# Rounding part of the in-projection weights on ScalarE in a Hymba-style hybrid decoder layer

## The chip, the cores and the metric

The kernel runs on one core of a Trainium2 chip. The metric is the device time of one execution in microseconds; three runs of the kernel before gave 2929.60, 2932.82 and 2933.56 us, median 2932.82.

TensorE is called PE below, VectorE DVE, ScalarE ACT, GpSimd POOL, and SyncE, which issues the transfers here, SP.

## The reference

One decoder layer over 2048 tokens of width 1024. A single in-projection feeds two parallel head groups, sparse attention and a Mamba-2 (SSD) mixer; their outputs go together through an out-projection, and an MLP of width 4096 follows.

```python
u = rms_norm(h, norm_pre_mix[i])
proj = u @ w_in[i]                      # 1024 x 2636
q, k, v, qi, ki, wi, z, xbc, dt = jnp.split(proj, offsets, axis=-1)
...
attn = sparse_attention(q, k, v, qi, ki, wi, rel_bias)   # top 256 keys by an indexer
ssd = ssd_mixer(z, xbc, dt, ...)                         # conv, chunked scan, gated norm
mix = jnp.concatenate([attn, ssd], axis=-1) @ w_out[i]
h = h + rms_norm(mix, norm_post_mix[i])
f = rms_norm(h, norm_pre_mlp[i]) @ w_mlp_up[i]
f = jnp.square(jax.nn.relu(f)) @ w_mlp_down[i]
h = h + rms_norm(f, norm_post_mlp[i])
```

## The kernel before

**Products.** Every large product is made of three: each operand is split into a high part, which is the value rounded to the format fp32r, and a low part, which is what the rounding left. PE multiplies high by high, high by low and low by high (`mm3`, lines 257, 260 and 261) and sums in PSUM.

**Weights.** `load_w` brings a weight tile in two parts. For each part SP issues the load of the raw tile `wr` (line 246), then `split` makes the high part `wh` (line 229 on ACT or line 231 on POOL, chosen by a flag) and then, always on POOL, the low part `wl = wr - wh` (line 232). `how` is a pair of characters, one flag for each part of a tile; "1" means ACT. There are two buffers for `wh`, two for `wl` and four for `wr`, so the pair of parts that PE works on fills `wh` and `wl`, and a part of the next tile can be rounded only when PE has done the 12 products of each kind that read the part it replaces. The flags of the four weight matrices stand in line 53 of the code as HI_ (in-projection), HO (out-projection), HU and HW (MLP).

**Stages.** The 2048 tokens are four pieces of 512 (t = 0 to 3). The in-projection takes them in order: for each t one narrow tile of mixed columns (`w_misc`, parts of 128x304) and 20 tiles of `w_in` (parts of 128x512): eight for x, B and C of the mixer, two for the indexer's queries, four for the gate z, one for K, one for V, four for the queries of the attention. Each tile is 24 products of 512 columns on PE. Then follow four windows, each an out-projection and an MLP for one t. `p_mm` is the PSUM tile of in-projection and MLP-up products, `p_acc` that of the out-projection, `p_dn` that of MLP-down.

**Work woven in.** Between the products of the in-projection (0 to 763 us in the trace) stand pieces of three other jobs: the SSD mixer of each t (lines 486 to 543), the search for the top 256 keys of query blocks 2 to 8 (`topk`: ACT counts with a Sign activation and an accumulator, line 611; DVE makes the next threshold from the count, lines 618 and 619; 31 steps in turn), and the attention of blocks 0 to 3 (lines 684 to 754). After the z tiles one activation (line 402) applies SiLU to 128x6144 values on ACT; then come the copies of K (line 414). At the end of each t, `row_scale` squares the next piece on ACT (line 283) and `moving` splits the next activations `u` on ACT, DVE and POOL (lines 305 to 312) from raw tiles `xr`, which share the four `wr` buffers.

**Order.** Each engine runs its own list in order; an instruction that waits holds up all behind it. The lists are laid out when the program is built, by a scheduler that places instructions by priority and by its own estimate of when their inputs are there. A changed engine for one operation therefore shifts other instructions too.

Of the kernel before, what the change touches and what calls it, by code (L numbers as in the profile page):

```python
# [41 lines left out]
def hybrid_layer(ctx, tc, x, x_t, w_cols, n_post_mix, n_post_mlp, w_in, w_misc, dt_bias, a_log, d_skip,  # L42
# [7 lines left out]
    dr = ctx.enter_context(tc.tile_pool(name="dr", bufs=1, space=DRAM))  # L50


    HI_, HO, HU, HW = "00,11,00,00".split(",")
    FC, BC = (2,3)
    TB = "acc"
    WL = 2
# [25 lines left out]
    def tl(tag, shape, dt=F32, name=None):  # L82
        pool, bufs, slot = place(tag)
        return pool.tile(shape, dt, tag=name if tag in ("s", "ks", "ssm") else slot, name=name or tag, bufs=bufs)
# [17 lines left out]
    def pt(tag, name=None):  # L102
        pool, bufs, slot = place(tag)
        return pool.tile([P, 512], F32, tag=slot, name=name or tag, bufs=bufs)
# [460 lines left out]
    def load_stack(r0, i, nh, tag):  # L565

        qs = tl(tag, [P, 2, nh, P], F32R, name=tag)
        for var in range(2):
            for part in range(2):
                SP.dma_start(qs[part * DH:(part + 1) * DH, var].bitcast(F32),  # L570
                                 q_d[part ^ var, r0:r0 + nh * DH, i * P:(i + 1) * P].rearrange("(h d) t -> d h t", d=DH))
        return qs

    def topk(i0, g):

        n = (i0 + g) * P
        per = g if g * n <= L else g // 2
        scs = []
        for i in range(i0, i0 + g):
            ni = (i + 1) * P  # L580
            qs = load_stack(0, i, HI, "qi")
            if len(scs) % per == 0:
                rows = tl("sc", [P, per, n])
            sc = rows[:, len(scs) % per, :]
            scs.append(sc)
            for j0 in range(0, ni, 512):
                w = min(512, ni - j0)
                for h in range(HI):
                    p = pt("tp", "p_ix")
                    for var in range(2):  # L590
                        PE.matmul(p[:, 0:w], qs[:, var, h, :], KI[:, j0:j0 + w], start=var == 0, stop=var == 1)  # L591
                    if h == 0:
                        V.tensor_scalar(sc[:, j0:j0 + w], p[:, 0:w], 0.0, wsc[:, i, 0:1], op0=OP.max, op1=OP.mult)
                    else:
                        S.activation(p[:, 0:w], p[:, 0:w], AF.Relu)
                        V.scalar_tensor_tensor(sc[:, j0:j0 + w], p[:, 0:w], wsc[:, i, h:h + 1], sc[:, j0:j0 + w],
                                               op0=OP.mult, op1=OP.add)
                yield
            V.tensor_tensor(sc[:, i * P:ni], sc[:, i * P:ni], cn["caus"], op=OP.add)
            if ni < n:  # L600
                G.memset(sc[:, ni:n], MASKED)

        cnt = tl("ks", [P, 4], name="cnt")[:, 0:g]

        keep = tl("ks", [P, 4], I32, name="keep")[:, 0:g]
        cnd = tl("ks", [P, 4], I32, name="cnd")[:, 0:g]

        def count(bias):

            for j in range(g):  # L610
                S.activation(junk_k[:, 0:n], scs[j], AF.Sign, bias=bias(j), accum_out=cnt[:, j:j + 1])  # L611

        count(lambda j: tiny)
        V.tensor_scalar(cnd, cnt, float(2 * TOPK - n), -1.0, op0=OP.is_lt, op1=OP.mult)
        V.tensor_scalar(cnd, cnd, -1073741824, None, op0=OP.bitwise_xor)
        for b in range(30, -1, -1):
            count(lambda j: cnd[:, j:j + 1].bitcast(F32))
            V.tensor_scalar(keep, cnt, float(2 * TOPK - n), float(1 << b), op0=OP.is_ge, op1=OP.mult)  # L618
            V.scalar_tensor_tensor(cnd, keep, (1 << b) | ((1 << b) >> 1), cnd, op0=OP.bitwise_xor, op1=OP.bitwise_xor)  # L619
            yield  # L620
        thr = tl("ks", [P, 4], name="thr")[:, 0:g]
        aux = tl("ks", [P, 4], name="aux")[:, 0:g]
        mag = tl("ks", [P, 4], I32, name="mag")[:, 0:g]
        V.tensor_scalar(mag, cnd, 0x7fffffff, None, op0=OP.bitwise_and)
        V.tensor_scalar(aux, mag.bitcast(F32), 1.17549435e-38, None, op0=OP.is_ge)
        V.tensor_tensor(mag.bitcast(F32), mag.bitcast(F32), aux, op=OP.mult)
        V.scalar_tensor_tensor(thr, cnd.bitcast(F32), -1.0, aux, op0=OP.mult, op1=OP.mult)
        V.tensor_scalar(aux, mag.bitcast(F32), float(2.0 ** -24 * (1 + 2.0 ** -10)), None, op0=OP.mult)
        for j in range(g):
            i, sc, t1, c1, a1 = i0 + j, scs[j], thr[:, j:j + 1], cnt[:, j:j + 1], aux[:, j:j + 1]  # L630
            mk = tl("mkk", [P, n], BF16)
            eq = junk_k[:, 0:n]
            V.tensor_scalar(mk, sc, t1, None, op0=OP.is_gt, op1=OP.add, accum_out=c1)
            V.scalar_tensor_tensor(a1, c1, float(TOPK), a1, op0=OP.is_ge, op1=OP.mult)
            V.tensor_tensor(t1, t1, a1, op=OP.add)
            V.tensor_scalar(mk, sc, t1, None, op0=OP.is_gt, op1=OP.add, accum_out=c1)
            V.tensor_scalar(c1, c1, -1.0, float(TOPK), op0=OP.mult, op1=OP.add)
            V.tensor_scalar(eq, sc, t1, -1.0, op0=OP.is_equal, op1=OP.mult)
            V.tensor_scalar(mk, sc, t1, -BIG, op0=OP.is_lt, op1=OP.mult)
            yield  # L640
            V.tensor_tensor_scan(sc, eq, eq, c1, op0=OP.add, op1=OP.bypass)
            V.scalar_tensor_tensor(sc, sc, 0.0, eq, op0=OP.is_lt, op1=OP.mult)
            V.scalar_tensor_tensor(mk, sc, BIG, mk, op0=OP.mult, op1=OP.add)
            SP.dma_start(m_d[i, :, 0:n], mk)
            yield
# [319 lines left out]
    def ktask(groups, a, b):  # L965
        n = sum(31 + sum(2 + -(-(i + 1) // 4) for i in range(i0, i0 + g)) for i0, g in groups)
        return "k", chain(*(topk(*e) for e in groups)), n, a, b
# [121 lines left out]
```

## Time and profile before

| | |
|---|---|
| median of three runs | 2932.82 us |
| the profiled execution | 2928.61 us |
| its span, first to last instruction | 2926.8 us |
| PE busy | 2754.8 us, 94% of the span |
| DVE, ACT, POOL busy | 1668.1, 1483.0, 1775.7 us |
| mean granted clock of PE | 0.977 of full speed |
| in-projection, from 0 to the first out-projection product | 763 us |

A row of the trace gives busy time of an engine, the time it sat idle before an instruction, and which engine's work ended that idle time. Matmuls overlap: in an undisturbed stretch a product of 512 columns is listed with 0.39 us, but one starts every 0.23 us.

### The profile page before, as it was taken

How to read it: one execution, taken by the hardware profiler on the slowest of the kernel's cores; microseconds unless marked ns; L12 is line 12 of the kernel's file. 1: busy time of each engine (PE TensorE's matmuls, PEld its weight loads, DVE VectorE, ACT ScalarE, POOL GpSimd, SP SyncE). 2: the span in 40 equal slices, each digit the busy share in tenths (PEclk: the TensorE clock that was granted, in tenths of full speed). 3: DMA queues.
4: the chain of work that ended last, by engine and by line, in shares of the span. 5: the costliest groups of instructions: out<-in, count | busy, mean ns of one | idle time of the engine just before them, and what ended most of it. 6: DMA issues, size and time to landing. Idle time of an engine off the chain costs nothing.

```text
span 2926.8 us, 41172 instructions
## 1 busy us (share of the span) xinstructions
PE 2754.8 (94%) x13558; PEld 2240.5 (77%) x13558; DVE 1668.1 (57%) x4106; ACT 1483.0 (51%) x2550; POOL 1775.7 (61%) x1721
## 2 busy tenths in 40 slices
PE   7988989888889999999899999999999999999998
PEld 5766767666668887888688878878888888778886
DVE  6579688878575656657765565666444342511113
ACT  2475577665746586767683847644332332311101
POOL 4666556667656656564457575644564656578775
PEclk9999999989989999999999999999999999999999
DMA  4754754634733333355233222553232225522222
GB/s 131 233 181 142 228 158 132 214 107 166 243 120 116 111 110 97 101 163 191 97 98 103 92 94 81 164 185 102 87 96 80 93 78 177 204 94 97 95 94 87
DMA packets 286741, 383.46 MB, mean 131 GB/s; under 512 B 26520, under 2 KB 151360, under 8 KB 286528
## 3 DMA queue, kind: packets, MB, share of 16 engines
q1 hardware_dynamic: 286528, 380.84, 40.1%
q8 instruction: 107, 1.75, 0.2%
q14 instruction: 106, 0.87, 0.1%
HBM read 316.44 MB, written 64.30 MB: 130 GB/s over the span
## 4 chain that ended last, share of the span: by engine, by line
PE 68%; DVE 13%; ACT 5%; DMA 5%; POOL 4%; issue 4%; SPq 1%; POOLq 0%; DVEq 0%; ACTq 0%
PE p_mm L261 9%; PE p_mm L257 9%; PE p_mm L260 9%; PE p_dn L261 7%; PE p_dn L260 7%; PE p_dn L257 7%; PE p_o L726 4%; PE p_s L684 4%; PE p_pt L718 3%; ACT junk_k L611 3%; POOL wl L232 2%; PE p_ix L591 2%; PE p_acc L257 1%; PE p_acc L260 1%; PE p_acc L261 1%
## 5 line engine op out<-in xcount | busy, mean ns | idle before, releaser
L232 POOL TENSOR_TENSOR wl<-wr,wh 128x512 fp32r<-128x512 f32 (+1 forms) x740 | 994.9, 1345 | 177.6 <-ACT wh L229 112.6
L231 POOL TENSOR_SCALAR wh<-wr 128x512 fp32r<-128x512 f32 x674 | 448.7, 666 | 727.6 <-PE p_mm L260 339.2
L257 PE MATMUL p_mm<-u,wh 128*128 128x512 f32 (+1 forms) x1696 | 680.4, 402 | 38.2 <-ACT u L311 15.4
L261 PE MATMUL p_mm<-u,wl 128*128 128x512 f32 (+1 forms) x1696 | 679.8, 402 | 13.6 <-POOL wl L232 13.5
L260 PE MATMUL p_mm<-u,wh 128*128 128x512 f32 (+1 forms) x1696 | 670.1, 396 | 0.5 <-POOL u L309 0.3
L611 ACT ACTIVATE junk_k<-sc,cnd 128x512 int8<-128x512 f32 (+10 forms) x434 | 576.4, 1328 | 161.7 <-DVE cnd L619 131.5
L260 PE MATMUL p_dn<-wl,g 128*128 128x512 f32 x1008 | 401.8, 399 | 3.5 <-POOL wl L232 3.5
L257 PEld LDWEIGHTS p_mm<-u,wh 128*128 128x128 f32 (+1 forms) x1696 | 321.3, 189 | 108.6 <-POOL wh L231 19.6
L261 PE MATMUL p_dn<-wh,g 128*128 128x512 f32 x1008 | 399.1, 396 | 2.7 <-POOL g L837 2.7
L261 PEld LDWEIGHTS p_mm<-u,wl 128*128 128x128 f32 (+1 forms) x1696 | 320.2, 189 | 88.4 <-POOL wl L232 22.0
L260 PEld LDWEIGHTS p_mm<-u,wh 128*128 128x128 f32 (+1 forms) x1696 | 320.6, 189 | 69.5 <-DVE u L312 2.1
L257 PE MATMUL p_dn<-wh,g 128*128 128x512 f32 x1008 | 328.7, 399 | 1.3 <-POOL wh L231 0.6
L835 ACT ACTIVATE r<-r 128x512 f32<-128x512 f32 x128 | 80.4, 629 | 434.6 <-DVE r L834 434.1
L689 DVE CUSTOM_DVE_ANT_0 pp<-p_s,mk 128x512 f32<-128x512 f32 (+3 forms) x320 | 192.7, 606 | 135.5 <-PE p_s L684 132.0
L720 ACT ACTIVATE ppt<-p_pt 128x512 fp32r<-128x512 f32 (+1 forms) x288 | 155.7, 567 | 209.4 <-PE p_pt L718 172.6
L721 DVE TENSOR_TENSOR ppt<-p_pt,ppt 128x512 fp32r<-128x512 f32 (+1 forms) x288 | 183.0, 654 | 120.8 <-ACT ppt L720 117.9
L260 PEld LDWEIGHTS p_dn<-wl,g 128*128 128x128 f32 x1008 | 189.9, 188 | 46.5 <-POOL wl L232 5.8
L261 PEld LDWEIGHTS p_dn<-wh,g 128*128 128x128 f32 x1008 | 190.0, 188 | 43.2 <-POOL g L837 3.1
L257 PEld LDWEIGHTS p_dn<-wh,g 128*128 128x128 f32 x1008 | 185.8, 189 | 41.9 <-POOL wh L231 2.9
L726 PE MATMUL p_o<-ppt,VV 128*128 128x256 f32 x1088 | 211.8, 295 | 1.1 <-ACT ppt L720 0.7
L618 DVE TENSOR_SCALAR keep<-cnt 128x1 int32<-128x1 f32 (+1 forms) x341 | 69.7, 204 | 234.9 <-ACT junk_k L611 233.5
L837 POOL TENSOR_TENSOR g<-r,g 128x512 fp32r<-128x512 f32 x128 | 170.1, 1330 | 54.4 <-ACT g L836 53.2
(252 smaller groups left out, 4209.6 us busy)
## 6 DMA issues: line engine op xcount, KB each, us to landing
wr<-w_up SPq DMA_DIRECT2D x256, 256.0 KB, 2.6
wr<-w_down SPq DMA_DIRECT2D x256, 256.0 KB, 2.6
wr<-w_in SPq DMA_DIRECT2D x160, 256.0 KB, 2.9
tq<-toep_d SPq DMA_DIRECT2D x128, 128.0 KB, 2.5
qs<-q_d SPq DMA_DIRECT2D x256, 64.0 KB, 2.4
wr<-w_out SPq DMA_DIRECT2D x64, 256.0 KB, 4.0
mix<-mix_d SPq DMA_DIRECT2D x32, 512.0 KB, 8.5
q_d<-qp SPq DMA_DIRECT2D x24, 512.0 KB, 3.8
```

Of the source, the lines that this page charges most:

```text
L231: G.tensor_scalar(dst_hi, src_f, 1.0, 0.0, op0=OP.mult, op1=OP.add)
L232: G.tensor_tensor(dst_lo, src_f, dst_hi.bitcast(F32), op=OP.subtract)
L257: m = PE.matmul(o, ah, bh, start=first, stop=False)
L260: PE.matmul(o, ah, bl, start=False, stop=False)
L261: state["mm3"] = PE.matmul(o, al, bh, start=False, stop=last).ins.name
L611: S.activation(junk_k[:, 0:n], scs[j], AF.Sign, bias=bias(j), accum_out=cnt[:, j:j + 1])
L684: PE.matmul(p[:, 0:w], qs[:, var, hh, :], K1[:, g, j0:j0 + w], start=var == 0, stop=var == 1)
L689: V.tensor_tensor_reduce(out=pp[:, j0:j0 + w], in0=p[:, 0:w], in1=mk[:, j0:j0 + w], scale=1.0, scalar=-3e38, op0=OP.add, op1=OP.max, accum ...
L720: S.activation(pg[:, 0, 0:w], p[:, 0:w], AF.Copy)
L721: V.tensor_tensor(pg[:, 1, 0:w], p[:, 0:w], pg[:, 0, 0:w].bitcast(F32), op=OP.subtract)
L726: PE.matmul(po[:, c0:c0 + 256], VV[:, kk, g, :], pg[:, part, j * 256:(j + 1) * 256], start=kk == 0 and part == 0, stop=kk == nb - 1 and pa ...
L837: G.tensor_tensor(gt[:, 1, :], r, gt[:, 0, :].bitcast(F32), op=OP.subtract)
```

## The change

In line 53 the flags of the in-projection go from "00" to "10": the high part of the first part of each in-projection weight tile is rounded by ACT (line 229) and no more by POOL (line 231). The second part stays with POOL, and so do both low parts. The narrow tile of t = 0 has flags of its own ("11") and stays as it was. In the built program 83 of POOL's 674 rounding instructions go to ACT, whose own go from 66 to 149; no other engine gets more or fewer instructions. A blank line is left out as well, so that from line 604 on each line number is one less.

```diff
-    HI_, HO, HU, HW = "00,11,00,00".split(",")
+    HI_, HO, HU, HW = "10,11,00,00".split(",")
...
         cnt = tl("ks", [P, 4], name="cnt")[:, 0:g]
-
         keep = tl("ks", [P, 4], I32, name="keep")[:, 0:g]
```

POOL's list in t = 0, at the first tiles of `w_in`, before (`wr` raw, `wh` high, `wl` low part):

```order
L231 TENSOR_SCALAR wh<-wr 128x512
L232 TENSOR_TENSOR wl<-wr,wh 128x512
L231 TENSOR_SCALAR wh<-wr 128x512
L232 TENSOR_TENSOR wl<-wr,wh 128x512
L231 TENSOR_SCALAR wh<-wr 128x512
L232 TENSOR_TENSOR wl<-wr,wh 128x512
```

And after:

```order
L231 TENSOR_SCALAR wh<-wr 128x512
L232 TENSOR_TENSOR wl<-wr,wh 128x512 x2
L231 TENSOR_SCALAR wh<-wr 128x512
L232 TENSOR_TENSOR wl<-wr,wh 128x512 x2
L231 TENSOR_SCALAR wh<-wr 128x512
L232 TENSOR_TENSOR wl<-wr,wh 128x512 x2
```

Of two high parts one is gone; the low part of a tile's first part now stands right behind the low part of the tile before.

ACT's list in t = 1, among the counts of the key search, after (line 610 is line 611 of before: the count; `pp` and `ppt` belong to the attention, `lm` and `cb` to the mixer):

```order
L610 ACTIVATE junk_k,cnt<-sc,cnd 128x512
L229 ACTIVATE wh<-wr 128x512
L736 ACTIVATE ot<-p_o 128x256
L610 ACTIVATE junk_k,cnt<-sc,cnd 128x512 x2
L698 ACTIVATE pp,den<-pp,nm 128x256
L610 ACTIVATE junk_k,cnt<-sc,cnd 128x512
L489 ACTIVATE lm<-lm,adt 128x128 x4
L490 ACTIVATE cb<-cb 128x512
L530 ACTIVATE si<-si 128x256
L610 ACTIVATE junk_k,cnt<-sc,cnd 128x512
L229 ACTIVATE wh<-wr 128x512
```

Between two rounding instructions there stand some ten others, five of them counts; before, none of the two L229 was there.

ACT's list in t = 2, around the long SiLU activation, before:

```order
L530 ACTIVATE si<-si 128x256
L402 ACT_TABLE_LOAD
L402 ACTIVATE pre<-pre 128x6144
L611 ACTIVATE junk_k,cnt<-sc,tiny 128x1024
L414 ACTIVATE K_84<-kk 64x512 x2
L611 ACTIVATE junk_k,cnt<-sc,tiny 128x1024
```

And after:

```order
L229 ACTIVATE wh<-wr 128x512
L402 ACT_TABLE_LOAD
L402 ACTIVATE pre<-pre 128x6144
L530 ACTIVATE si<-si 128x256
L229 ACTIVATE wh<-wr 128x512
L414 ACTIVATE K_84<-kk 64x512 x2
L229 ACTIVATE wh<-wr 128x512
```

The high part of the K tile now stands ahead of the SiLU, that of the V tile behind it.

## Rows read from the trace of the kernel before

**Rows 1.** The page: busy time, share of the span, instructions of each engine

```profile
PE 2754.8 (94%) x13558; PEld 2240.5 (77%) x13558; DVE 1668.1 (57%) x4106; ACT 1483.0 (51%) x2550; POOL 1775.7 (61%) x1721
```

**Rows 2.** By stage: length, busy time of each engine, PE clock, DMA share, GB/s

```profile
45.00:763.00 718.00, 632.78 (x3152) 494.10 (x3152) 560.36 (x1405) 442.99 (x911) 461.54 (x458) 0.96 0.54 171
...
1200.00:2926.00 1726.00, 1676.74 (x8217) 1386.16 (x8215) 812.65 (x1897) 744.36 (x1128) 1029.17 (x984) 0.99 0.35 115
```

**Rows 3.** PE's waits, 45 to 763 us: for whom, us in total, times, longest

```profile
PE p_mm L257 <- POOL wh L231: 11.0, 9, 6.4
PE p_mm L261 <- POOL wl L232: 6.5, 13, 1.1
PE p_y L514 <- DVE ends L492: 6.2, 2, 3.3
PE p_s L684 <- DVE mx L689: 5.3, 5, 2.2
...
PE p_pt L718 <- ACT pp L699: 4.6, 4, 2.5
```

**Rows 4.** POOL by line, 0 to 763 us: busy, mean ns, idle before and releasers

```profile
L232 POOL TENSOR_TENSOR wl<-wr,wh 128x512 fp32r<-128x512 f32 x162 | 221.6, 1369 | 12.7 <-PE p_mm L261 1.0
L231 POOL TENSOR_SCALAR wh<-wr 128x512 fp32r<-128x512 f32 x160 | 111.1, 695 | 115.0 <-PE p_mm L260 93.4 <-DMA wr<-w_in 13.9 <-issue 7.5
```

**Rows 5.** Timeline of POOL in t = 0: start, us, instruction, idle before it

```profile
66.13 0.63 POOL L231 TENSOR_SCALAR wh<-wr 128x512 fp32r<-128x512 f32 x1 [0.71 <-PE p_mm L260]
66.84 1.60 POOL L232 TENSOR_TENSOR wl<-wr,wh 128x512 fp32r<-128x512 f32 x1
68.85 0.62 POOL L231 TENSOR_SCALAR wh<-wr 128x512 fp32r<-128x512 f32 x1 [0.41 <-PE p_mm L260]
```

**Rows 6.** Timeline of PE: two of its waits for a high part

```profile
464.91 0.50 PE L257 MATMUL p_mm<-u,wh 128*128 128x512 f32 x1 [1.46 <-POOL wh L231]
```

```profile
589.06 0.71 PE L257 MATMUL p_mm<-u,wh 128*76 128x512 f32 x1 [6.40 <-POOL wh L231]
```

**Rows 7.** Timelines of SP's queue and of POOL ahead of the wait at 589 us

```profile
584.94 4.01 SPq L246 DMA_DIRECT2D wr<-w_misc  x2
```

```profile
588.57 0.44 POOL L231 TENSOR_SCALAR wh<-wr 128x304 fp32r<-128x304 f32 x1
```

**Rows 8.** DVE by line, 0 to 763 us

```profile
L374 DVE SCALAR_TENSOR_TENSOR pre<-raw,cols,pre 128x512 f32<-128x512 f32 x96 | 88.6, 924 | 3.0 <-ACT pre L372 2.1
L619 DVE SCALAR_TENSOR_TENSOR cnd<-keep,cnd 128x2 int32<-128x2 int32 x93 | 35.4, 380 | 1.4
L618 DVE TENSOR_SCALAR keep<-cnt 128x2 int32<-128x2 f32 x93 | 32.0, 344 | 43.5 <-ACT junk_k L611 43.2
```

**Rows 9.** Lines 374 and 619, 0 to 763 us: ns least, median, most

```profile
L374 DVE SCALAR_TENSOR_TENSOR pre<-raw,cols,pre x96: 714/749/1787, 41.0 to 672.9; 128x512 f32<-128x512 f32 x96
```

```profile
L619 DVE SCALAR_TENSOR_TENSOR cnd<-keep,cnd x105: 143/160/1256, 133.8 to 761.6; 128x2 int32<-128x2 int32 x93, 128x1 int32<-128x1 int32 x12
```

**Rows 10.** Line 229, and what engines at tile p_acc waited for (us, times)

```profile
L229 ACT ACTIVATE wh<-wr x66: 456/623/635, 4.1 to 2528.8; 128x512 fp32r<-128x512 f32 x64, 128x304 fp32r<-128x304 f32 x2
...
  POOL wl L232: 112.6, 46
```

```profile
  POOL wl L232: 3.0, 7
...
  ACT wh L229: 1.9, 3
```

**Rows 11.** Timelines of ACT and DVE around the SiLU of t = 2

```profile
534.72 5.35 ACT L402 ACTIVATE pre<-pre 128x6144 f32<-128x6144 f32 x1 [3.51 <-DVE pre L329]
```

```profile
541.61 0.68 DVE L329 TENSOR_TENSOR kk<-p_mm,rsb 128x512 f32<-128x512 f32 x1
```

**Rows 12.** ACT by line and DVE's longest wait, 0 to 763 us

```profile
L611 ACT ACTIVATE junk_k<-sc,cnd 128x1024 int8<-128x1024 f32 x62 | 70.9, 1144 | 31.1 <-DVE cnd L619 26.8 <-DVE cnd L615 2.0 <-DVE rs_q L219 0.8
```

```profile
DVE keep L618 <- ACT junk_k L611: 50.4, 44, 2.7
```

## The prediction

> **What bounds the kernel now.** The first view is the page's line of busy times: PE is busy for 94% of the span [rows 1], so its products set the length, and a change that moves no product can only move PE's idle time. The second is the table by stage [rows 2]: from 1200 us on PE is busy 97% of the time, but from 45 to 763 us only 632.8 of 718 us, 85 us idle in the very stage that the change touches, at a granted clock of 0.96. The third is the list of PE's waits there [rows 3]. Its 36 rows sum to 80 us: rows ended by DVE sum to 48, by POOL to 17.5, by DMA to 7, by ACT to 6. The reader is to see two things. The two rows on weights, 11.0 and 6.5 us, are all that POOL's weight work costs PE directly, so they bound the direct gain. And the largest share is DVE's, which runs in turn with ACT: its longest wait is for ACT's counts, 50.4 us [rows 12]. ACT is at 443 of 718 us there, POOL at 462, DVE at 560 [rows 2].
>
> The sum is made against the profiled execution, 2928.6 us with a span of 2926.8. That is 4.2 us under the median of the three runs, so 4.2 is added at the end.
>
> **Where the rounding stands now.** In t = 0, before other work is woven in, POOL makes a high part in 0.62 us and a low part in 1.3 to 1.6, then waits 0.41 or 0.71 us for PE to free the next buffer; a part goes by every 2.72 us [rows 5], and PE waits for none. Later POOL also has the mixer's and the attention's work, and comes late 22 times [rows 3]. Over the stage it still waited 93.4 us for PE to free a buffer [rows 4]: mostly it is early.
>
> **The change, part by part.** 80 parts of 128x512 and three of 128x304 move. *What POOL saves* is 83 x 0.62 = 51 us, some 11% of its 462 us in the stage. What of it PE sees is in the two rows on weights. The 6.4 us at 589 us [rows 6] is no rounding: SP stood for 4.0 us over the two loads of that tile's raw parts [rows 7], and the rounding itself was 0.44 us. That leaves 21 waits of 11.1 us in total, the longest 1.46 [rows 6], most around 0.6 us. A queue that is one high part shorter takes at most 0.62 us off each, which cuts five that are longer to a rest of 2 us together: at most 9 us off. Only one part in two is relieved directly; the other finds a shorter queue ahead. I take -6, between 0 and -9.
>
> *What DVE saves.* Small DVE operations are slow in this stage. Line 619 works on two numbers per partition and takes 143 ns at the least, 160 at the median, 1256 at the most [rows 9], 380 in the mean [rows 8]; in the timelines the long ones are those that begin while POOL is at work, and end when it ends. The excess over the short ones is (380 - 160) x 93 = 20 us there, (344 - 160) x 93 = 17 us for line 618 and (924 - 749) x 96 = 17 us for line 374 [rows 8, 9]: 54 us in three groups, perhaps 90 in all, an estimate by the same reading of the smaller groups of that view. POOL's time falls by 11%, so DVE saves 6 to 10 us. PE sees it only where a DVE result is what it waits for, 48 us of 718: from next to nothing (-0.5) to all of it (-10). I take -2, nearer the low end, since most of DVE's small operations are followed by a count on ACT, not by PE.
>
> *What ACT gets.* The same copy takes ACT 0.62 us [rows 10], so 51 us more on 443, 62% to 69% of the stage. Directly PE waits for ACT 6 us; DVE waits for it some 95 us, of which the counts are half [rows 12]. Lengthened by 51/443 = 12%, that is 0.7 us of PE's and 11 us of DVE's; the second is again passed on only in part. Bounds 0 and +12; I take +2, by the same share as for DVE. The Trainium skill (ScalarE: Activation LUTs, Rules for kernel authors) budgets about 0.3 us plus 0.83 ns per element for one activation, which for 512 elements would be 0.73 us and 60 us in all; the row has 0.62, and with 0.73 this term would grow by a fifth, to +2.4.
>
> *What the handover costs.* The new wait is POOL's low part on ACT's high part; queued behind it on POOL are the second part's rounding, the mixer's products (lines 501 to 523) and `qp`. No row shows it in this stage, but the out-projection does it for all of its 64 parts: there POOL waited 112.6 us in 46 waits for ACT, 1.76 us a part, and yet the engines at `p_acc` waited only 1.9 us for the high and 3.0 us for the low parts [rows 10], 0.08 us a part. For 83 parts that would be +6 with PE's weight loads counted in, +2 or so for PE alone. Apart from that there is one place per t that has no likeness in the out-projection: the SiLU of 5.35 us with its table load, behind which V's high part now stands in t = 0, 2 and 3. In t = 2 it ends at 540.1 us; after the 0.4 us of line 530 and 0.62 us of rounding the high part is there at 541.0, the low part at 542.4. K's products are done by 541.6, when DVE takes their sum [rows 11], and V's low part is wanted two products (0.46 us) later, at 542.1: 0.3 us late. In t = 0 and 3 the same reckoning gives 0.4 and 0. So +1 for the three, +9 if each is 3 us late. Together I take +3, between 0 and +15.
>
> *The order.* All lists shift a little from t = 0 on. It moves no work between stages: the in-projection of t = 2 ends at the same place in PE's list as before (2207 instructions from its start) and that of t = 3 twelve later, with one more mixer step ahead of it. A single stall in the stage is 1 to 6 us [rows 3, 6], and which of them stay is chance: 0, with 5 either way. A wait also costs clock: after the wait of 6.4 us a product is listed with 0.71 us where 0.39 is usual [rows 6]; it goes with the waits and is inside those 5.
>
> The sum: -6 - 2 + 2 + 3 = **-3 us**. 2928.6 - 3 = 2925.6 and, moved to the median, **2930 us**. What measurement can tell from no change is 0.2%, 5.9 us, so this is a forecast of no measurable difference.
>
> **The rivals.** *Slower: ACT's list holds the high part back.* A first part may be rounded when PE has done its predecessor, and its low part is wanted 2.72 + 0.46 us later; less 0.62 and 1.3 us of work, 1.3 us are free. ACT serves its list in order, and in t = 2 and 3 that is full of counts of 1024 columns, 1.14 us each and in pairs [rows 12]. The lateness read off the out-projection is 1.76 - 0.62 = 1.1 us a part, just inside the 1.3; from there every microsecond goes to PE. At 0.4 us beyond it on the 42 parts of t = 2 and 3 it costs 17 us, with 3 us at the SiLUs 20; less the 8 saved, +12: 2945. For it: two engines must now be on time, and ACT is the one that others wait for. Against it: 0.08 us a part in the out-projection [rows 10].
>
> *Faster: DVE's stalls count in full.* If the 10 us that DVE saves all lie ahead of PE's 48 us of waits for DVE, the sum is -6 - 10 + 2 + 3 = -11: 2922; with the handover at 0 and POOL's 9 in full, -17: 2916. For it: DVE is the busiest helper of the stage and ends most of PE's waits. Against it: the low parts stay on POOL, and they are two thirds of its weight work and hit DVE for twice as long each. The Trainium skill (SBUF — State Buffer, Who interferes with whom) says that GpSimd and VectorE share one pair of ports under an exclusive lock, that the later one blocks fully, and that ScalarE never waits on anyone; the spread in rows 9 agrees with that, and by that rule alone the move is a gain of this size.
>
> *The change does nothing to PE:* every wait for POOL becomes one for ACT of the same length, 2933. It falls into the forecast's band.
>
> **How the numbers follow.** Forecast and its like (2927 to 2938): 0.40. Slower rival, 2939 to 2950: 0.27. Faster rival, 2914 to 2927: 0.33. The range leaves out the ends of both: 2917 to 2946. Faster by over 0.2%: 0.33; within: 0.40; slower: 0.27.
>
> **What the profile after would show.** POOL's busy time in the first 763 us down by about 51 us, ACT's up by as much. PE's waits for `wh` on POOL down to the 6 us at 589, with a new row `wh` on ACT; that row under 4 us speaks for the forecast, over 12 for the slower rival. The mean of lines 618 and 619 (617 and 618 after) down by a tenth; by a third, with the DVE rows of PE's waits shorter, for the faster one. The start of the out-projection, at 763 us now, at 755 to 768; the stages behind it of the same length within 3 us. The forecast is wrong if that start moves by more than 6 us, or if the time moves behind it, which no term here holds.

## The result: slower by 0.59%

The changed kernel took 2947.13 us (median of 6 runs, 2945.08 to 2956.44), the kernel before 2931.82 us (6 runs, the three given at the start among them, 2925.67 to 2937.26). The ratio is 1.0059, with a 95% interval of 1.0044 to 1.0073. The forecast was 2930 us and no measurable difference; the time lies 17 us above it and 1 us above the range. The profiled execution after took 2945.26 us, with a span of 2943.5.

The first rows of after answer to [rows 1] and [rows 2]: busy time, share and instructions of each engine over the span, then the two stretches (length, busy time of PE, PEld, DVE, ACT and POOL, clock, DMA share, GB/s).

```profile
PE 2764.2 (94%) x13558; PEld 2245.6 (76%) x13558; DVE 1654.7 (56%) x4106; ACT 1519.0 (52%) x2633; POOL 1723.8 (59%) x1638
...
45.00:763.00 718.00, 637.48 (x3185) 498.78 (x3184) 551.01 (x1395) 470.85 (x977) 413.13 (x380) 0.95 0.54 172
1200.00:2926.00 1726.00, 1677.82 (x8189) 1382.95 (x8188) 794.58 (x1837) 729.41 (x1107) 1032.10 (x986) 0.99 0.34 114
```

The instructions moved as said: 83 fewer on POOL and 52 us less of its time, 83 more on ACT and 36 us more (the 83 roundings sum to some 51 us; on ACT neighbouring rows overlap in part). In the stretch that the change touches PE is even busier than before, 637.5 against 632.8 us.

The list of PE's waits from 45 to 763 us answers to [rows 3] (for whom, us in total, times, longest).

```profile
PE p_mm L261 <- POOL wl L232: 14.4, 21, 2.2
PE p_y L514 <- DVE ends L492: 8.1, 1, 8.1
...
PE p_mm L257 <- ACT wh L229: 4.1, 5, 2.0
```

The waits for high parts fell from 11.0 to 4.1 us and those for low parts rose from 6.5 to 14.4: on weights PE waited 17.5 us before and 18.5 after. And here is why, in POOL's and ACT's groups from 0 to 763 us (busy and mean ns, then the idle time before them and what ended it), to be read against [rows 4]:

```profile
L232 POOL TENSOR_TENSOR wl<-wr,wh 128x512 fp32r<-128x512 f32 x161 | 222.5, 1383 | 157.3 <-ACT wh L229 133.8 <-PE p_mm L261 4.9 <-DMA qi<-q_d 4.8
L231 POOL TENSOR_SCALAR wh<-wr 128x512 fp32r<-128x512 f32 x80 | 57.3, 716 | 56.2 <-issue 35.7 <-POOL wl L232 7.8 <-DMA toep_d<-toep 4.8
...
L229 ACT ACTIVATE wh<-wr 128x512 fp32r<-128x512 f32 x81 | 50.3, 621 | 31.2 <-PE p_mm L260 17.0 <-POOL wl L232 7.6 <-issue 6.2
```

Before, the largest share of POOL's idle time was 93 us of waiting for PE to free a buffer, that is, of being early. Now it waits 134 us for ACT's high parts. PE's 21 waits for a low part can be told apart by what POOL did just ahead of that part. In 11 of them, 5.0 us together, POOL had stood for ACT's high part. In eight others, 8.6 us together, it came without a gap from a product of the mixer (lines 501, 504, 523). One of these, in the timelines of POOL and PE after:

```profile
669.42 1.49 POOL L504 TENSOR_TENSOR cb<-cb,si 128x512 f32<-128x512 f32 x1 [3.49 <-DMA si<-s_d]
670.87 1.26 POOL L232 TENSOR_TENSOR wl<-wr,wh 128x512 fp32r<-128x512 f32 x1
```

```profile
672.19 0.50 PE L261 MATMUL p_mm<-u,wl 128*128 128x512 f32 x1 [0.98 <-POOL wl L232]
```

So PE still waits for POOL's own queue, and waits for ACT's are added to it. That the waits for high parts fell is mostly the wait of 6.4 us for `w_misc` [rows 6], which is gone; but hardly any time was won by that. PE came to this place later, behind a wait of 8.1 us for DVE where it had waited 3.3 before, and the first product of `w_misc` starts at 588.0 us against 589.1. Timeline of PE after:

```profile
580.86 0.66 PE L514 MATMUL p_y<-lm,xd 128*64 128x128 f32 x2 [8.14 <-DVE ends L492]
...
588.01 0.71 PE L257 MATMUL p_mm<-u,wh 128*76 128x512 f32 x1 [0.28 <-ACT wh L229]
```

In the whole list of PE's waits in this stretch, the rows ended by DVE sum to 36 us (48 before), those by ACT to 15 (6), those by POOL to 15 (17.5), and all rows to 79 (80). The waits went from DVE to ACT, and the sum stayed.

**Where the time went.** The two traces can be laid side by side by PE's work: for each moment of before, the moment at which after has done the same amount of products (an estimate worked out from the two timelines of PE, each product with its time in an undisturbed stretch). After against before:

| us of before | 225 | 425 | 676 | 775 | 875 | 1326 | 1575 | 1875 | 1970 | 2875 |
|---|---|---|---|---|---|---|---|---|---|---|
| lag, us | +8.2 | +0.6 | -3.5 | -4.9 | +2.1 | +1.4 | +10.7 | +10.7 | +16.3 | +16.3 |

In this pair the in-projection ends with a gain, 7 us are lost between 775 and 875 us, and the rest in three steps up to 1970 us; from there to the end nothing changes. So the whole loss stands behind the stage that was changed, where no operation went to another engine. One thing is mixed into these numbers: of the 16.7 us between the two spans, 7.3 are idle time of PE and 9.4 are busy time, since the same 13558 products ran at a mean granted clock of 0.973 of full speed against 0.977. In the other executions on record the clock was 0.972 to 0.979 before and 0.971 to 0.977 after, so a part of the lag may belong to these two executions and not to the kernels.

The first step is the handover of window 0: the out-projection is done, and the MLP cannot start until DVE has made the residual `xh` (line 802 before, 801 after) and the MLP's operands `u` (line 810 and 809). Timeline of PE before (start, us, instruction, idle before it): the last out-projection product and the first of MLP-up.

```profile
823.65 0.39 PE L261 MATMUL p_acc<-wh,mix 128*128 128x512 f32 x1
...
851.52 0.50 PE L257 MATMUL p_mm<-u,wh 128*128 128x512 f32 x1 [0.33 <-DVE u L810]
```

After:

```profile
822.86 0.39 PE L261 MATMUL p_acc<-wh,mix 128*128 128x512 f32 x1
...
850.54 3.68 PE L806 MATMUL p_tr<-ident,xh 128*128 128x128 f32 x16 [4.47 <-DVE u L809]
...
854.94 0.61 PE L257 MATMUL p_mm<-u,wh 128*128 128x512 f32 x1
```

27.9 us before, 32.1 after. The same stretch by engine, before and after (length, busy time of PE, PEld, DVE, ACT and POOL, clock, DMA share, GB/s):

```profile
823.90:851.50 27.60, 15.43 (x89) 11.65 (x87) 27.12 (x67) 9.36 (x25) 12.51 (x10) 0.69 0.45 159
```

```profile
823.10:854.90 31.80, 18.13 (x91) 14.07 (x91) 31.28 (x90) 15.19 (x36) 8.43 (x10) 0.58 0.34 121
```

DVE is busy for 27.1 of 27.6 us before and for 31.3 of 31.8 after. It sets the length of this stretch, and it has 4.2 us more to do. PE stands idle for 12.2 us of it before and for 13.7 after; the rest of its 4.2 us is that its products run slower, at a mean granted clock of 0.58 against 0.69 of full speed, a mix of its two levels of 1.2 and 2.4 GHz. What DVE did meanwhile, before (its timeline, the rows over 1152 columns):

```profile
816.56 1.41 DVE L633 TENSOR_SCALAR_CACHE_REDUCE mkk<-sc,thr 128x1152 bf16<-128x1152 f32 x1
...
824.05 2.60 DVE L641 TENSOR_TENSOR_SCAN sc<-junk_k,cnt 128x1152 f32<-128x1152 int8 x1
826.69 1.58 DVE L642 SCALAR_TENSOR_TENSOR sc<-sc,junk_k 128x1152 f32<-128x1152 f32 x1
830.51 1.57 DVE L643 SCALAR_TENSOR_TENSOR mkk<-sc,mkk 128x1152 bf16<-128x1152 f32 x1
```

And after:

```profile
837.65 1.40 DVE L635 TENSOR_SCALAR_CACHE_REDUCE mkk<-sc,thr 128x1152 bf16<-128x1152 f32 x1
...
845.12 2.60 DVE L640 TENSOR_TENSOR_SCAN sc<-junk_k,cnt 128x1152 f32<-128x1152 int8 x1
...
848.48 1.34 DVE L641 SCALAR_TENSOR_TENSOR sc<-sc,junk_k 128x1152 f32<-128x1152 f32 x1
849.75 2.71 DVE L809 SCALAR_TENSOR_TENSOR u<-p_tr,cols,u 128x512 fp32r<-128x512 f32 x4
852.72 1.34 DVE L642 SCALAR_TENSOR_TENSOR mkk<-sc,mkk 128x1152 bf16<-128x1152 f32 x1
```

These are the last seven passes of the key search of query block 8 (`topk`, lines 633 to 643 before): they make its mask, which the attention of that block reads later and the MLP does not. Before, four of the seven are over when the out-projection ends. After, all seven, 9.7 us of DVE, lie between the last out-projection product and the first of MLP-up. The place was to be read in DVE's list, of which the diff shows nothing. Before, all seven stand ahead of the first `xh` (the two ends of the piece; the number in front is the line of the list):

```
1480 L633 TENSOR_SCALAR mkk_7527,cnt_5651<-sc_5516,thr_7519 128x1152
...
1496 L643 SCALAR_TENSOR_TENSOR mkk_7527<-sc_5516,mkk_7527 128x1152
...
1512 L802 SCALAR_TENSOR_TENSOR xh_8076<-o_8072,rs1_8878,xh_8076 128x256 x3
```

After, six of the seven stand among `xh` and `u`:

```
1512 L632 TENSOR_SCALAR mkk_7527,cnt_5651<-sc_5516,thr_7519 128x1152
1522 L801 SCALAR_TENSOR_TENSOR xh_8076<-o_8072,rs1_8878,xh_8076 128x256 x3
...
1544 L641 SCALAR_TENSOR_TENSOR sc_5516<-sc_5516,junk_k_79 128x1152
1545 L809 SCALAR_TENSOR_TENSOR u2_8918<-p_tr_8913,cols_75,u2_8918 128x512
...
1550 L642 SCALAR_TENSOR_TENSOR mkk_7527<-sc_5516,mkk_7527 128x1152
```

The key search runs in turn between DVE's threshold and ACT's count. Its counts stand in the same ACT list as the 83 new roundings. It comes later now: the first pass of block 8 starts 53 us after the first out-projection product before, and 70 us after it now. That this delay is the roundings' own, and not the work of the scheduler that laid out the lists anew, is not shown; with the move in t = 3 alone (e12 below) the pass comes earlier than before, 40 us after that product.

### The profile page after: what moved, and what is told of

Same layout as the page of the kernel before. It is cut to its first block, busy times and chain, and to the rows that moved or that the text cites. A ratio compares the mean times of both kernels' runs of the same rounds, so it can differ in the third digit from the quotient of the medians.

```text
span 2943.5 us, 41198 instructions
## 1 busy us (share of the span) xinstructions
PE 2764.2 (94%) x13558; PEld 2245.6 (76%) x13558; DVE 1654.7 (56%) x4106; ACT 1519.0 (52%) x2633; POOL 1723.8 (59%) x1638
## 4 chain that ended last, share of the span: by engine, by line
PE 69%; DVE 12%; DMA 5%; issue 5%; POOL 4%; ACT 3%; SPq 1%; POOLq 0%; DVEq 0%; ACTq 0%
PE p_mm L261 10%; PE p_mm L257 9%; PE p_mm L260 9%; PE p_dn L260 7%; PE p_dn L261 7%; PE p_dn L257 7%; PE p_o L725 4%; PE p_s L683 4%; PE p_pt L717 4%; POOL wl L232 2%; ACT junk_k L610 2%; PE p_ix L591 1%; DVE pre L374 1%; PE p_acc L257 1%; PE p_acc L260 1%
## 5 line engine op out<-in xcount | busy, mean ns | idle before, releaser
L231 POOL TENSOR_SCALAR wh<-wr 128x512 fp32r<-128x512 f32 (+1 forms) x591 | 396.6, 671 | 679.4 <-PE p_dn L261 331.8
L833 DVE SCALAR_TENSOR_TENSOR r<-p_mm,rsb 128x512 f32<-128x512 f32 x128 | 88.0, 689 | 211.7 <-PE p_mm L261 183.8
```

Source lines behind the costliest of these rows:

```text
L231: G.tensor_scalar(dst_hi, src_f, 1.0, 0.0, op0=OP.mult, op1=OP.add)
```

## The experiments

Times are medians; "to before" is the difference to the kernel before as it ran beside that kernel.

### The stage by itself

Both kernels, cut off after the in-projection; copies of the first 128 rows of the input are written out in place of the rest.

```diff
     front.close()
-    state["win"] = "1"
...
-    weave(window(3), [])
```

> The kernel before cut off behind the in-projection stage with the work woven into it: no window, no MLP; the output is 16 copies of rows of x and stands for nothing. It gives the stage a time of its own, some 840 us by the trace (the mixer's last steps end at about 835 us). To be compared with e6 alone.

> The kernel after the change, cut in the same way; the difference to e5 is what the moved rounding does to the stage itself. Theory A (later lists): between -10 and +3 us, since by equal work on PE the profiled run after is 4 us ahead at 775 us. Theory B (the rounding itself): +10 or more.

Measured: 879.38 us for before (875.78 to 881.62), 867.46 after (865.41 to 869.86): 12 us faster with the move. The longest wait of the cut kernel before, 10.3 us for a high part of `w_misc` at the place where the whole kernel before waits 6.4 us [rows 6], is not in the other one. Timelines of PE and POOL there:

```profile
585.90 0.71 PE L257 MATMUL p_mm<-u,wh 128*76 128x512 f32 x1 [10.29 <-POOL wh L231]
```

```profile
585.40 0.44 POOL L231 TENSOR_SCALAR wh<-wr 128x304 fp32r<-128x304 f32 x1 [4.59 <-DMA wr<-w_misc]
```

POOL itself waited there for the load; the rounding is 0.44 us. But this wait is not what the changed kernel gains. There PE comes to the same product at the same time without it, having waited just before for the mixer (5.1, 1.2 and 1.0 us from 574 us on, where the cut kernel before has no other wait). Timeline of PE in e6:

```profile
586.04 0.77 PE L257 MATMUL p_mm<-u,wh 128*76 128x512 f32 x1
```

By equal work of PE (an estimate as above, from the two timelines) it is 1 to 3 us ahead at 600 us, and it gets a lead of some 17 us between there and 680 us, where the cut kernel before has waits of 4.3 and 3.5 us for DVE's results (lines 329 and 225). What follows is only that the move does not make the stage longer; to what the gain belongs is not shown.

### The same comparison in other orders

If the loss belongs to the move, it must stay when the order of the windows is changed by an edit that has nothing to do with it. Four such edits were made to both kernels. Each changes a place in the program from which a task is woven in, adds no operation, and leaves TensorE's list as it is up to the MLP of window 0 or further.

```diff
-    K3, C1, C2, C3 = (-40,760),(-50,355),(355,740),(10,380)
+    K3, C1, C2, C3 = (-30,760),(-50,355),(355,740),(10,380)
```

That is e1 and e2. In e3 and e4 K3 is (-40,740), in e13 and e14 (-50,760); in e15 and e16 C1 and C2 are (-50,365),(365,740).

> The kernel before, with one number of the later weave changed: the key search of blocks 9 to 15 starts at 30 instead of 40 units ahead of the windows. The lists of the in-projection stay word for word as they are on PE; no instruction is added, taken away or moved to another engine. Theory A (the 15 us come from where the later windows' lists happen to put their pieces, not from the rounding): this harmless edit moves the time too, by up to 15 us either way. Theory B (ACT's extra rounding in the in-projection makes the loss): 2932 within 6 us.

> The same number changed in the kernel after the change. Theory A: the difference to the kernel before is no longer +15; anything from -10 to +25, and the difference to e1 too. Theory B: 2947 within 6 us, 15 above e1.

> The kernel before with the end of the same search at 740 instead of 760 units. Theory A: again a shift of up to 15 us either way, of another size than in e1. Theory B: 2932 within 6 us.

> The same in the kernel after the change. Theory A: the difference to e3 is anything from -10 to +25 and not the same as between e2 and e1. Theory B: 2947 within 6 us, 15 above e3.

> The kernel before with the key search of blocks 9 to 15 started ten units earlier in the program (-50 in place of -40): TensorE's list is the same up to the MLP of window 0, no operation is added. Theory (chance of the order behind 850 us): any edit of the order there costs time, because the order of the kernel before happens to be a good one: 2935 to 2955. Rival (the order is worth little): 2930 to 2936, as the kernel before.

> The changed kernel with the same edit. Theory (the move's own loss is the handover of window 0, 5 us; the rest is chance of the order): 0 to 10 us from the kernel before with this edit, on either side of 5; handover 92 to 94 us here against 88. Rival (the move has a loss of 12 or more behind the in-projection of its own): 12 to 20 us above.

> The kernel before with the attention of blocks 5 to 11 ten units later in the program (365 in place of 355): the list is the same up to about 1000 us. Theory (chance of the order): 2935 to 2955. Rival (the order is worth little): 2930 to 2936.

> The changed kernel with the same edit. Theory (handover of 5 us plus chance): 0 to 10 us from the kernel before with this edit. Rival (a loss of its own of 12 or more): 12 to 20 us above.

Measured, with the order as given first:

| order | before, to before | after, to before | after less before |
|---|---|---|---|
| as given | 0 | +15.3 | +15.3 |
| K3 (-30,760): e1, e2 | +12.7 | +23.0 | +10.3 |
| K3 (-40,740): e3, e4 | +1.6 | +21.4 | +19.8 |
| K3 (-50,760): e13, e14 | +31.4 | +25.7 | -5.7 |
| C1 (-50,365): e15, e16 | +8.6 | +19.3 | +10.7 |

Two things follow. An edit that does no work moves the kernel before by 2 to 31 us, always up (the 1.6 of e3 is within the noise): of the five orders its own is the best. And the move costs 10 us in the mean of the five, with a standard error of 4 (from the five differences, which scatter by 9.6 about their mean); from five differences that gives a 95% interval from about -2 to 22, so a loss in every order is likely but not certain. e13 and e14 went against both theories stated for them, with the changed kernel the faster one, and the difference of e15 and e16 lies between the two theories.

The start of the out-projection does not carry the loss. With the C1 pair, the K3 pairs and e7 and e8 (below), six executions on either side share TensorE's list up to there. The first out-projection product comes at 763.4 to 770.1 us in those of before (mean 766.0) and at 761.5 to 774.0 in those of after (mean 767.6). The gain of 2 us in the profiled pair (763.6 to 761.5) is inside that scatter. Nor did the products end earlier. The last in-projection product comes 5 us later after (761.08 against 756.13); before, PE then stood for a transfer of `mix`, which is not so after. Timeline of PE before:

```profile
756.13 0.39 PE L261 MATMUL p_mm<-u,wl 128*128 128x512 f32 x1
...
763.59 1.62 PE L257 MATMUL p_acc<-wh,mix 128*128 128x512 f32 x3 [5.39 <-DMA mix<-mix_d]
```

After:

```profile
761.08 0.39 PE L261 MATMUL p_mm<-u,wl 128*128 128x512 f32 x1
...
761.55 1.06 PE L257 MATMUL p_acc<-wh,mix 128*128 128x512 f32 x3
```

The handover does carry a loss. From the last out-projection product of window 0 to the first of MLP-up the six executions of before take 27.8, 27.9, 28.0, 28.1, 28.3 and 28.3 us, the six of after 31.9, 31.9, 32.0, 32.0, 32.1 and 32.1. The other end repeats too, at no cost: between the last in-projection product and the first of the out-projection the six of before take 4.9 to 7.5 us and the six of after 0.5 to 0.6, but the last in-projection product comes later in those of after, and the out-projection starts no earlier.

### The passes out of the handover

In e9 and e10 six of the seven passes are left out for block 8 alone, so that its mask isn't exact.

```diff
-            V.tensor_scalar(mk, sc, t1, None, op0=OP.is_gt, op1=OP.add, accum_out=c1)
...
+            if i0 != 8:
+                V.tensor_scalar(mk, sc, t1, None, op0=OP.is_gt, op1=OP.add, accum_out=c1)
...
+            else:
+                V.tensor_scalar(mk, sc, t1, -BIG, op0=OP.is_lt, op1=OP.mult)
+                yield
```

> The kernel before, with the key search's last passes (lines 633 to 643) left out for query block 8 alone, so that this block's mask is not exact and the output means nothing. Theory (handover): between the first out-projection product of window 0 and the first MLP-up product PE lives on what VectorE makes; the seven passes over 1152 columns, some 10 us of VectorE, cost PE about 5 us when they stand in that stretch and nothing when they stand ahead of it, as in the kernel before. So here that stretch stays at 88 to 89 us (before: 87.9) and the time within 0.3% of the kernel before. Rival (chance of the order, everywhere): the stretch may be anything from 88 to 94.

> The changed kernel with the same passes of block 8 left out (output means nothing). In the changed kernel they stand among VectorE's instructions for the handover, and the stretch from the first out-projection product to the first MLP-up product takes 93.4 us. Theory (handover): it falls to 88 to 89 here, and the distance to the kernel before falls from 15 to 10 us. Rival (chance of the order): it stays at 92 to 94, since the passes are not its cause.

Measured: 2952.87 us for before (+15.8), 2946.93 for after (+9.8). Timeline of PE in e10, the two ends of the handover:

```profile
823.00 0.39 PE L261 MATMUL p_acc<-wh,mix 128*128 128x512 f32 x1
...
847.92 0.48 PE L257 MATMUL p_mm<-u,wh 128*128 128x512 f32 x1
```

24.9 us, where the changed kernel takes 32.1; in e9 it is 26.7, where the kernel before takes 27.9. From the first out-projection product it is 84.6 us, less than the 88 to 89 expected, and 87.5 in e9. DVE's busy time in this stretch of e10 is 22.7 us, against 31.3. The passes are the cause of the longer handover: without them that of the changed kernel is no longer than the other's. In the whole time e10 is 6 us below e9, and 10 above the kernel before, as expected of it. That e9 came out 16 us above the kernel before, by leaving work out, is put down here to the chance of the order once more, without a run that shows it; it had been expected within 0.3%.

In e17 and e18 the whole search of block 8 goes to the windows, with all of the computation kept.

```diff
-    K0 = 9
+    K0 = 8
```

> The kernel before with the key search of block 8 taken out of the in-projection and put ahead of that of block 9 in the windows, so that its passes stand behind the first handover. Theory (handover): the stretch from the first out-projection product to the first MLP-up product is 85 to 89 us, as before; the time depends on the order of the windows, 2930 to 2955.

> The changed kernel with the same edit. Theory (handover): the stretch is 85 to 89 us here too, the loss of 5 us is gone, and what is left of the move is the gain of the in-projection: the time is 10 us under to 3 us over that of the kernel before with this edit. Rival (a loss of its own in the windows): 8 to 15 us above.

Measured: 2944.11 us for before (10 runs, 2939.04 to 2950.17) and 2944.33 for after (10 runs, 2939.99 to 2951.61), a difference of 0.2. From the first out-projection product to the first of MLP-up it is 83.6 us in e17 and 79.6 in e18, less than the 85 to 89 expected; between the last out-projection product and that, 23.5 and 25.3. With the handover free of the passes in both, the move costs nothing and gains nothing in this pair; by the scatter of 9.6 us above, one pair does not settle it. Both are slower than the kernel before by 9 us, so this is no version to keep.

### Parts of the move

```diff
     def in_proj(t):
         t0 = t * T
+        HI_ = HIS if t in (1, 2,) else "00"
```

with `HIS` the flags "10", and in e12 `t in (3,)`.

> The move for t = 1 and 2 alone; in t = 0 and 3 GpSimd rounds as before. In VectorE's list the passes of block 8 stand ahead of the handover again. Theory (handover, with a real gain inside the in-projection): the stretch from the first out-projection product to the first MLP-up product takes 88 to 89 us; the loss of about 9 us in t = 0 is not made and the gain of t = 1 and 2 stays, so the out-projection begins at 754 to 760 us; the time is 2922 to 2935. Rival (the move costs time wherever it is made, by the longer ScalarE list): the out-projection begins at 762 or later and the time is 2938 to 2948.

> The move for t = 3 alone; the passes of block 8 stand ahead of the handover in VectorE's list. Theory (handover): the stretch from the first out-projection product to the first MLP-up product takes 88 to 89 us, the out-projection begins at 758 to 764, the time is 2924 to 2936. Rival (the move costs time wherever it is made): a quarter of the whole loss, 2936 to 2940, with a stretch of 89 to 91.

Measured: 2961.09 us for t = 1 and 2 (+24.0), 2951.41 for t = 3 (+14.3): neither theory's time. A part of the move costs as much as the whole or more, which no account by tiles allows. On the handover the two fall out as the place of the passes says. In e11 they run from 824 to 842 us, all behind the last out-projection product (824.0), and PE takes 34.6 us from there; so the expectation of a free handover was wrong, because it was read from DVE's list, where they stand ahead of the first `xh`, and not from when they run. In e12 they run from 811 to 825 us, ahead of that product (830.6), and PE takes 22.1, the shortest of all. So the move alone does not put the passes into the handover; the order that comes with it does.

### The passes of blocks 9 to 15 out

In e7 and e8 the passes are left out for the blocks whose search runs in the windows (their masks aren't exact).

```diff
-            V.tensor_scalar(mk, sc, t1, None, op0=OP.is_gt, op1=OP.add, accum_out=c1)
...
+            if i0 < 9:
+                V.tensor_scalar(mk, sc, t1, None, op0=OP.is_gt, op1=OP.add, accum_out=c1)
...
+            else:
+                V.tensor_scalar(mk, sc, t1, -BIG, op0=OP.is_lt, op1=OP.mult)
+                yield
```

> The kernel before without the passes that settle ties in the key search of blocks 9 to 15 (lines 632 to 643 but for one comparison), which leaves out part of the computation. These passes read two SBUF operands on DVE over up to 2048 columns, and POOL's rounding of the MLP weights is up to three times as long beside them. Both theories: faster than before by 10 to 25 us.

> The same passes left out of the kernel after the change. Theory A1 (the later loss is made by these passes meeting POOL's MLP weights at other places): the difference to e7 shrinks to between -6 and +5 us. Theory A2 (the later loss has other causes in the later lists): it stays anywhere, +15 among them. Theory B: +15 as before.

Measured: 2918.16 us for before (-15.8), 2921.60 for after (-12.3), a difference of 3.4 where the kernels as given have 15.3. So leaving out passes that no product of the MLP reads gained 16 us, in spite of a changed order. The 3.4 us are about the handover's 4.1, which is left in this pair. The pair was made to see whether the passes collide with the weights of the MLP on POOL. Timeline of POOL in the changed kernel, in the MLP of window 1, beside the passes of block 13 (which run from 1530 to 1551 us):

```profile
1539.66 7.02 POOL L232 TENSOR_TENSOR wl<-wr,wh 128x512 fp32r<-128x512 f32 x2
...
1549.12 2.91 POOL L232 TENSOR_TENSOR wl<-wr,wh 128x512 fp32r<-128x512 f32 x1
1552.00 0.62 POOL L231 TENSOR_SCALAR wh<-wr 128x512 fp32r<-128x512 f32 x1
1552.70 1.30 POOL L232 TENSOR_TENSOR wl<-wr,wh 128x512 fp32r<-128x512 f32 x1
```

A low part takes 3.5 us beside the passes and 1.3 us behind them, and PE has two waits for one there, 2.4 and 1.8 us. It is one of the steps of the lag (5.7 us between 1525 and 1575). But in the kernel before the same blocks meet too, with a low part of 4.74 us at 1540, and PE was not waiting just then. Whether the fall from 15.3 to 3.4 us is due to these meetings or to chance, one pair cannot tell, since pairs scatter by 9.6.

## Why the prediction was wrong

The step that failed is the order's, "It moves no work between stages": the whole loss came up behind the stage, where no term of the sum stands (the last of the parts below). Inside the stage the sum came out, by luck: the forecast had -3 us, and PE's waits there went from 80 to 79, but its terms were mis-sized one by one and made up for each other.

**POOL's part (-6) was too large.** The bound was right, 17.5 us of waits; the step that failed is "a queue that is one high part shorter takes at most 0.62 us off each", taken as a gain on most of them. Without the wait for `w_misc`, PE waited 11.1 us for parts behind POOL's queue before. After, 9.4 us of its waits are for low parts ahead of which POOL had not stood for ACT, most of them straight behind the mixer's products: some 2 us less, not 6. The wait of 6.4 us that was to stay did go, but PE spent it on DVE instead.

**The handover of weights (+3) was too small.** PE waited 4.1 us for high parts on ACT, just over the forecast's own mark of 4, and 5.0 us for low parts that POOL could not begin because ACT's high part was late: 9 us, inside its bounds of 0 to 15. Right behind the SiLU a high part came 2.0 us late in t = 3 and a low part 0.6 in t = 2, against +1 for the three. The slower rival as it was named, ACT holding the high parts back, did not happen: its mark was 12 us.

**DVE's part (-2) was too small, and its sign was right.** The three groups that it was worked out from did not get shorter. Lines 374, 618 and 619 [rows 8], now 374, 617 and 618, by line from 0 to 763 us:

```profile
L374 DVE SCALAR_TENSOR_TENSOR pre<-raw,cols,pre 128x512 f32<-128x512 f32 x96 | 94.0, 983 | 7.2 <-ACT pre L372 6.5
L617 DVE TENSOR_SCALAR keep<-cnt 128x2 int32<-128x2 f32 x93 | 34.6, 372 | 44.6 <-ACT junk_k L610 44.2
L618 DVE SCALAR_TENSOR_TENSOR cnd<-keep,cnd 128x2 int32<-128x2 int32 x93 | 33.0, 355 | 1.5
```

They sum to 161.6 us, against 156.0 before. But DVE's busy time over the whole span fell from 1668.1 to 1654.7 us for the same 4106 instructions, and it is lower with the move in each of the four other orders, by 5 to 23 us; so a saving of about the size forecast (6 to 10 us) is there, in other groups. And PE's waits for DVE in the stage fell by 12 us, more than the bound of 10; in all five orders they are 30 to 38 us with the move and 45 to 50 without. The Trainium skill (SBUF — State Buffer, Who interferes with whom) says that VectorE and GpSimd share a pair of ports under an exclusive lock and that the later one blocks fully. The low parts of 3.5 us above agree with that; how much of the 13 us saved is due to it, no run here shows.

**ACT's longer queue (+2) was too small in the stage, and looked no further.** The working asked how much PE's and DVE's waits for ACT would grow inside the in-projection. DVE's longest, for counts, did not grow (50.4 us before, 45.7 after), but PE's waits for ACT rose from 6 to 15 us (15 to 23 against 6 to 7 over the five orders), 4.1 of them for the high parts above. And behind the stage, the search as a whole ended 17 us later against the out-projection, and its last passes fell into a stretch behind the in-projection in which PE lives on DVE. What they cost there, 4 us, is shown by e9 and e10 and by the six executions on either side; that ACT's longer queue brought them there is not.

**The order (0, with 5 either way) was mis-sized most.** "It moves no work between stages" was read from PE's list, and is right for PE's products. DVE's list shows the passes going over into the handover. And 5 us is far too small for chance behind the in-projection: the kernel before moved by 2 to 31 us under edits that add nothing. The start of the out-projection moved by 2 us, inside the 6 allowed; but "if the time moves behind it, which no term here holds" came true with the whole loss.

**What stays open.** Of the 15 us, 4 are the handover. The move's loss over five orders is 10 us with a standard error of 4. The 6 beyond the handover can't be told from zero, and in the two pairs in which the handover is free the difference is +0.2 and -5.9. In the profiled pair PE's waits behind 860 us grew from 45.8 to 52.4 us, those for POOL's weight parts (lines 231 and 232) alone from 13.5 to 22.0; but in e3 and e4, where the move costs most, the latter are 16.7 and 16.4, so this does not carry the loss from order to order. The rest of the 15 is most likely that the kernel before has a good order, the best of its five, which any change loses. This was not shown, and none of the three steps of the lag behind 1326 us has a cause that a run shows.

## What to carry to other kernels

- Where each engine's list is laid out by a scheduler, a change of engine is judged by what goes over the border of a stage on every engine, not on the bottleneck alone. Look first for the stretches in which the bottleneck lives on a helper, such as a handover from one product to the next, and at what else that helper's list holds there.
- Taking work off an engine that mostly waits for buffers brought little here (some 2 us of PE's waits), and the new engine's list made other parts late (9 us). What shares that list, above all a chain of small steps in turn (here 31 counts), is to be looked at as a whole: where does it end now?
- A wait that is gone is no gain by itself. Compare the time at which the same product starts: twice here a long wait had only changed places with one ahead of it.
- Before a difference of half a per cent is put down to a change, make the comparison again under two or three edits that only shuffle the order; with a spread like this one a single pair decides nothing.

## What the runs showed that was not expected

- Executions with one and the same list of TensorE up to there differ by up to 6.7 us at the start of the out-projection (763.4 to 770.1 us), though the handover behind it repeats to 0.5 us.
- The passes of the key search that e7 leaves out in blocks 9 to 15 take 92 us of DVE (1668.1 us before, 1576.5 in e7), and leaving them out brings 16 us, although no product of the MLP reads their results.
- POOL's low part of 128x512 takes 1.3 us alone and 3.5 us beside these passes.
